# The second MLP matrix of a Fourier-mixer block by seven block products, with the sums in DRAM

## Chip, cores and metric

One core of a Trainium2 chip. The metric is device time of one execution in microseconds (us). The kernel before takes 1678.18 us, the median of three runs (1675.69 to 1680.62).

## The reference, cut to what matters

One layer over 512 tokens of width 2048, batch 1, float32. The change touches the last line but one alone: the product with `w_mlp_out`.

```python
def sqrelu_mlp(h, w1, w2):
    return jnp.square(jax.nn.relu(h @ w1)) @ w2          # 2048 -> 8192 -> 2048
...
y_lat = fourier_mix(h_lat) @ fnet_w_out[slot]            # FFT over tokens and groups of 256
x = x + g1 * rms_norm(y_lat, norm_g[i, 1])
x = x + g2 * rms_norm(sqrelu_mlp(modulate(rms_norm(x, norm_g[i, 2]), sh2, sc2), w_mlp_in[i], w_mlp_out[i]), norm_g[i, 3])
return x
```

## The kernel before

**Three products for one.** Every float32 operand of TensorE is split in two: ScalarE writes a rounded copy `hi` (L115) and VectorE the rest `lo` = source - `hi` (L116). `mm3` (L118 to L121) multiplies hi x lo, lo x hi and hi x hi into one PSUM bank. Weights come by `stream` (L632): a 512 KB load on SP's queue into one of eight buffers `raw`. A weight tile of 128 x 1024 thus costs one load, one CAST on ScalarE and one TENSOR_TENSOR on VectorE.

**First MLP matrix.** The 8192 hidden features are 64 blocks of 128, taken in 32 pairs (units). Pairs 0 to 3 are made together, 4 and 5 by `unit_plain` (L823: 96 matmuls with 512 columns), 6 to 31 by `unit` (L775): token halves, halves of the width and the two blocks of the pair make a 2 x 2 by 2 x 2 block product, which needs seven products (A11, S1, S3, S2, A12, A22, S4) in place of eight, so 168 matmuls with 256 columns, and sums of weights on VectorE (L795, L800, L803, L806). `square_out` (L641) squares on ScalarE and writes the pair's 512 KB from GpSimd's queue to a DRAM tile `gd` (L643).

**Second MLP matrix.** `CHUNKS` cuts the 64 blocks into seven chunks of 8 and two of 4. At a chunk's start `g_in` (L855) loads its pairs back and splits them. For each of the four column groups of 512, 8 blocks x 4 token tiles x 3 = 384 matmuls of 512 columns run per chunk with four PSUM banks; ScalarE copies the banks of chunk 0 into `oacc` (L882), VectorE adds those of the other chunks to it (L884). The last chunk (60, 64) is made token tile by token tile, with the norm and the output behind each (L906 to L928).

**What sets the order.** Each engine runs its instructions in the order in which the program's scheduler put them; an instruction waits for semaphores of other engines and of DMAs. The tile pools have fixed numbers of buffers (8 `raw`, 3 `hi`, 3 `lo`, 6 PSUM banks for products); a buffer that is taken again makes its next writer wait for its last reader. `owed` and `settle` put an eviction off until the next product has been issued.

Of the kernel before, what the change touches and what calls it, by code (L numbers as in the profile page):

```python
# [12 lines left out]
ALU = mybir.AluOpType  # L13
# [42 lines left out]
def block_kernel(ctx: ExitStack, tc, xs, c_l, w_mod, b_col, g_col,  # L56
                 w_in_a, w_in_b, w_in_s, w_out, wf, wf_nyq, fmat_a, fmat_b, csmat, altmat, identm, out):
    nc = tc.nc
# [585 lines left out]

# [178 lines left out]
    def unit_plain(u):  # L823
        pss = []
        for j in range(2):
            ps = bank()
            for half in range(2):
                wr = stream(w_in_b[2 * (u - WAVE // 2) + j, half].rearrange("p k f -> p (k f)"))
                wh, wl = hi4([P, 8, P]), lo4([P, 8, P])
                split(wh, wl, wr.rearrange("p (k f) -> p k f", f=P))  # L830
                for i in range(8):
                    dt = half * 8 + i
                    mm3(ps, wh[:, i, :], wl[:, i, :], hh[dt // 4][:, dt % 4, :], hl[dt // 4][:, dt % 4, :], dt == 0, dt == KT - 1)
            pss.append(ps)
        act_relu2(u, pss)

    for u in range(WAVE // 2, UNIT0):
# [5 lines left out]
        unit_plain(u)  # L843
    for u in range(UNIT0, UNITS):
# [7 lines left out]
    oacc = [x8([P, D]) for _ in range(4)]  # L852
    gts = {}

    def g_in(u):  # L855
        gr = stream(gd[u].rearrange("p f t -> p (f t)"))
        for j in range(2):
            gh, gl = g2k([P, 512], F32R), g2k([P, 512], F32R)
            split(gh, gl, gr[:, j * 512:(j + 1) * 512])
            gts[2 * u + j] = (gh, gl)  # L860

    for c, (f0, f1) in enumerate(CHUNKS):
        for u in range(f0 // 2, f1 // 2):
            g_in(u)
        if c == len(CHUNKS) - 1:
            break
        for n in range(4):
            ns = slice(n * 512, (n + 1) * 512)
            ps = [bank() for _ in range(4)]
            for fb in range(f0, f1, 2):  # L870
                wr = stream(w_out[fb // 2, n].rearrange("p f j -> p (f j)"))
                wh, wl = hi4([P, 2, 512]), lo4([P, 2, 512])
                split(wh, wl, wr.rearrange("p (f j) -> p f j", j=512))
                for i in range(2):
                    fi = fb + i
# [131 lines left out]
```

## Time and profile before

| what | value |
|---|---|
| median of three runs | 1678.18 us (1675.69 to 1680.62) |
| profiled execution, its own time | 1679.38 us |
| span of the profiled execution | 1677.6 us |
| mean granted TensorE clock | 0.992 of full speed |
| matmuls | 10161 |
| HBM read, written | 279.58 MB, 25.17 MB |

The span is what lies between the first and the last instruction of the trace; the execution's own time is 1.8 us longer. Of the views, the shares of busy time tell which engine is full, the chain of waits tells which engine's work the end is made of, the lines tell how long one instruction of a kind takes, the windows tell the same by stage, and the timeline gives start times, from which the spacing of matmuls is read (they are pipelined, so a matmul's own length is more than it costs).

### The profile page before, as it was taken

How to read it: one execution, taken by the hardware profiler on the slowest of the kernel's cores; microseconds unless marked ns; L12 is line 12 of the kernel's file. 1: busy time of each engine (PE TensorE's matmuls, PEld its weight loads, DVE VectorE, ACT ScalarE, POOL GpSimd, SP SyncE). 2: the span in 40 equal slices, each digit the busy share in tenths (PEclk: the TensorE clock that was granted, in tenths of full speed). 3: DMA queues.
4: the chain of work that ended last, by engine and by line, in shares of the span. 5: the costliest groups of instructions: out<-in, count | busy, mean ns of one | idle time of the engine just before them, and what ended most of it. 6: DMA issues, size and time to landing. Idle time of an engine off the chain costs nothing.

```text
span 1677.6 us, 24773 instructions
## 1 busy us (share of the span) xinstructions
PE 1637.5 (98%) x10161; PEld 1392.7 (83%) x10161; DVE 1046.3 (62%) x1417; ACT 658.3 (39%) x989; POOL 22.8 (1%) x46
## 2 busy tenths in 40 slices
PE   6999998999999999999999999999999999999997
PEld 4766654678999999999999988888888888888886
DVE  6777866675988888888777732344343434343557
ACT  6443334335555555454555533222122313221322
POOL 0000000000000000000000000000000000000000
PEclk9999998999999999999999999999999999999999
DMA  9888888886355555554433453424242424342542
GB/s 365 328 299 320 296 306 300 298 312 227 114 177 190 183 179 181 185 177 169 133 126 126 163 164 113 134 98 146 100 143 96 151 99 141 100 150 89 176 149 101
DMA packets 83698, 306.37 MB, mean 183 GB/s; under 512 B 9540, under 2 KB 9556, under 8 KB 82560
## 3 DMA queue, kind: packets, MB, share of 16 engines
q1 hardware_dynamic: 78480, 286.96, 49.7%
q0 software_dynamic: 5104, 17.83, 2.8%
q8 instruction: 79, 1.29, 0.3%
q14 instruction: 35, 0.29, 0.1%
HBM read 279.58 MB, written 25.17 MB: 182 GB/s over the span
## 4 chain that ended last, share of the span: by engine, by line
PE 94%; DMA 3%; DVE 2%; ACT 0%; issue 0%; SPq 0%; DVEq 0%; ACTq 0%
PE ps L119 19%; PE ps L121 18%; PE ps L120 18%; PE ps L789 10%; PE ps L788 10%; PE ps L790 10%; PE mv L202 4%; DMA raw<-in_w_mod 2%; PE mv L168 1%; DMA x<-in_xs 1%; DVE row L217 1%; PE mv L398 0%; PE ps L274 0%; DVE big L485 0%; DVE lo L116 0%
## 5 line engine op out<-in xcount | busy, mean ns | idle before, releaser
L116 DVE TENSOR_TENSOR lo<-raw,hi 128x1024 fp32r<-128x1024 f32 x326 | 398.4, 1223 | 380.4 <-ACT hi L115 370.0
L115 ACT CAST hi<-raw 128x1024 fp32r<-128x1024 f32 x326 | 342.4, 1051 | 593.1 <-PE ps L121 348.5
L119 PE MATMUL ps<-lo,g 128*128 128x512 f32 x1088 | 425.4, 392 | 0.3 <-DVE lo L116 0.3
L120 PE MATMUL ps<-hi,g 128*128 128x512 f32 x1088 | 425.0, 391 | 0.0
L121 PE MATMUL ps<-hi,g 128*128 128x512 f32 x1088 | 421.5, 391 | 0.0
L119 PEld LDWEIGHTS ps<-lo,g 128*128 128x128 f32 x1088 | 204.7, 188 | 49.1 <-issue 3.9
L121 PEld LDWEIGHTS ps<-hi,g 128*128 128x128 f32 x1088 | 204.5, 188 | 46.4 <-issue 4.1
L120 PEld LDWEIGHTS ps<-hi,g 128*128 128x128 f32 x1088 | 204.6, 188 | 43.9 <-issue 1.9
L789 PE MATMUL ps<-big,lo 128*128 128x256 f32 x624 | 177.1, 284 | 0.0
L788 PE MATMUL ps<-big,hi 128*128 128x256 f32 x624 | 176.9, 283 | 0.0
L790 PE MATMUL ps<-big,hi 128*128 128x256 f32 x624 | 176.6, 283 | 0.0
L789 PEld LDWEIGHTS ps<-big,lo 128*128 128x128 f32 x624 | 119.7, 192 | 0.5 <-DVE lo L116 0.2
L788 PEld LDWEIGHTS ps<-big,hi 128*128 128x128 f32 x624 | 119.7, 192 | 0.0
L790 PEld LDWEIGHTS ps<-big,hi 128*128 128x128 f32 x624 | 119.8, 192 | 0.0
L789 PE MATMUL ps<-g,lo 128*128 128x256 f32 x416 | 118.0, 284 | 0.0
L789 PE MATMUL ps<-s,lo 128*128 128x256 f32 x416 | 117.7, 283 | 0.0
L790 PE MATMUL ps<-s,hi 128*128 128x256 f32 x416 | 117.7, 283 | 0.0
L788 PE MATMUL ps<-g,hi 128*128 128x256 f32 x416 | 117.7, 283 | 0.0
L788 PE MATMUL ps<-s,hi 128*128 128x256 f32 x416 | 117.7, 283 | 0.0
L790 PE MATMUL ps<-g,hi 128*128 128x256 f32 x416 | 117.7, 283 | 0.0
L202 PE MATMUL mv<-raw,cst 128*32 128x256 f32 x1088 | 88.9, 406 | 11.1 <-DMA raw<-in_w_mod 7.2
L884 DVE TENSOR_TENSOR x<-x,ps 128x512 f32<-128x512 f32 x112 | 74.6, 685 | 27.7 <-PE ps L121 27.7
(225 smaller groups left out, 2223.7 us busy)
## 6 DMA issues: line engine op xcount, KB each, us to landing
raw<-in_w_mod SPq DMA_DIRECT2D x192, 512.0 KB, 5.2
raw<-in_w_out SPq DMA_DIRECT2D x128, 512.0 KB, 3.5
raw<-in_w_in_s SPq DMA_DIRECT2D x104, 512.0 KB, 3.7
raw<-in_wf SPq DMA_DIRECT2D x32, 512.0 KB, 6.2
gd<-tmp POOLq DMA_DIRECT2D x32, 512.0 KB, 3.1
raw<-gd SPq DMA_DIRECT2D x32, 512.0 KB, 3.2
raw<-in_w_in_a SPq DMA_DIRECT2D x16, 512.0 KB, 4.7
x<-in_xs SPq DMA_DIRECT2D x4, 1024.0 KB, 9.4
```

The source lines that it names most:

```text
L115: nc.scalar.copy(out=hi, in_=src)
L116: nc.vector.tensor_tensor(out=lo, in0=src, in1=as32(hi), op=ALU.subtract)
L119: nc.tensor.matmul(ps, lhsT=ah, rhs=bl, start=start, stop=False)
L120: nc.tensor.matmul(ps, lhsT=al, rhs=bh, start=False, stop=False)
L121: nc.tensor.matmul(ps, lhsT=ah, rhs=bh, start=False, stop=stop)
L168: nc.tensor.matmul(mv[:, 256 + cb:257 + cb], lhsT=rows[:, cb * P:(cb + 1) * P], rhs=ones[:, 0:1], start=True, stop=True)
L202: nc.tensor.matmul(st["ps"][32 * j:32 * j + 32, 0:256], lhsT=cst[:, kq * 4 + j, :], rhs=t[:, j * 256:(j + 1) * 256], start=(kq == 0), stop ...
L217: nc.vector.scalar_tensor_tensor(out=rows, in0=t[:, j * 512:(j + 1) * 512], scalar=sil[:, kt:kt + 1], in1=rows, op0=ALU.mult, op1=ALU.add)
L788: nc.tensor.matmul(ps, lhsT=wh[:, ks], rhs=ll, start=start and k == 0, stop=False, skip_group_check=True)
L789: nc.tensor.matmul(ps, lhsT=wl[:, ks], rhs=lh, start=False, stop=False, skip_group_check=True)
L790: nc.tensor.matmul(ps, lhsT=wh[:, ks], rhs=lh, start=False, stop=k == 7, skip_group_check=True)
L884: nc.vector.tensor_add(out=oacc[t][:, ns], in0=oacc[t][:, ns], in1=ps[t])
```

## The change

Chunks 0 to 6 (pairs 0 to 27) of the second matrix are now made by the same seven block products. The left matrix's 2 x 2 blocks are token halves (`T0`, `T1`) by two halves of the chunk's features; the right one's are feature halves by column halves of 512. For each chunk and each of two column groups `j`, `second(c, j)` makes seven products of 24 matmuls with 512 columns (4 feature blocks x 2 token tiles x 3), so 336 per chunk. Per chunk there are

- 16 weight loads as before (28 splits of weights, since sums of weights are split too), 16 weight sums on VectorE of 128 x 1024;
- 2 loads of 1 MB of activations (`g_chunk`), 4 sums on VectorE for S1, S3, S2, S4 and 7 splits (`left_in`), which serve both `j`; those of the next chunk are issued behind the products that `NEXT` names;
- 28 evictions by ScalarE of 128 x 512 into a ring of six buffers `ev`, and 14 DMAs of 512 KB from GpSimd's queue to 14 DRAM tiles `pacc` (one for each product and `j`). For chunk 0 they are plain, for the six others they add to what is there (`accum_op`): 84 accumulating DMAs.

After the last chunk `gather(j)` loads seven sums of 512 KB and VectorE combines them into `oacc`. Then LAST[0] = (56, 60) runs as a chunk did before, with column groups in the order 0, 2, 1, 3 and `gather(1)` ahead of group 1, and LAST[1] = (60, 64) with the output as before. The pool `bp` of the front is closed before the second matrix and its space goes to three new pools. Pair 31 is made by `unit_plain`, not by `unit`; `gd` now holds four pairs to a tile (the rows that `square_out` writes are 2 KB instead of 4 KB). The host only lays out the weights in another order.

```diff
+PLAIN = tuple(range(WAVE // 2, UNIT0)) + (UNITS - 1,)
+CHUNKS = 7
+LAST = ((56, 60), (60, 64))
...
-    gd = [dp.tile([P, 2, 512], F32, name=f"gd{u}") for u in range(UNITS)]
+    gd = [dp.tile([P, 2, 4, 512], F32, name=f"gd{c}") for c in range(UNITS // 4)]
...
-        nc.gpsimd.dma_start(out=gd[u], in_=r)
+        nc.gpsimd.dma_start(out=gd[u // 4][:, :, u % 4, :], in_=r)
...
+    unit_plain(UNITS - 1)
+    front.close()
+    g4p = ctx.enter_context(tc.tile_pool(name="g4p", bufs=6, reuse_waits="tile"))
+    sbp = ctx.enter_context(tc.tile_pool(name="sbp", bufs=5, reuse_waits="tile"))
+    sap = ctx.enter_context(tc.tile_pool(name="sap", bufs=8, reuse_waits="tile"))
...
+    def g_chunk(c):
+        gf = [s8(True, [P, 4, 512], F32) for _ in range(2)]
+        for j in range(2):
+            nc.sync.dma_start(out=gf[j].rearrange("p u t -> p (u t)"), in_=gd[c][:, j].rearrange("p u t -> p (u t)"))
+        raws[c]["g"] = gf
+    def left_in(c, s):
...
+        a11, a21, a12, a22 = gf[0][:, :, T0], gf[0][:, :, T1], gf[1][:, :, T0], gf[1][:, :, T1]
...
+        elif s == "S1":
+            src = st["v"] = tmp4([P, 4, 256])
+            nc.vector.tensor_sub(out=src, in0=a22, in1=a21)
...
+        t = s8(s in ("A11", "S1", "S3"), [P, 2, 4, 256], F32R)
+        split(t[:, 0], t[:, 1], src)
+        left[c][s] = t
+    def second(c, j):
...
+        def product(s, src):
+            ps = [bank(), bank()]
+            for h in range(2):
+                wh, wl = hi4([P, 1024]), lo4([P, 1024])
+                split(wh, wl, src[h])
+                for k in range(2):
+                    ks = slice(k * 512, (k + 1) * 512)
+                    for i in range(2):
+                        ts = slice(i * P, (i + 1) * P)
+                        t = left[c][s]
+                        mm3(ps[i], t[:, 0, 2 * h + k, ts], t[:, 1, 2 * h + k, ts], wh[:, ks], wl[:, ks], h + k == 0, h + k == 2)
+            settle()
+            def out():
+                ev = g4([P, 2, 512])
+                for i in range(2):
+                    nc.scalar.copy(out=ev[:, i, :], in_=ps[i])
+                if c:
+                    nc.gpsimd.dma_start(out=pacc[s, j], in_=ev, accum_op=ALU.add)
+                else:
+                    nc.gpsimd.dma_start(out=pacc[s, j], in_=ev)
+            owed.append(out)
+            if c + 1 < CHUNKS:
+                for n in NEXT.get((j, s), ()):
+                    left_in(c + 1, n)
+        b11, b12 = load(0), load(1)
+        product("A11", b11)
+        both = [g4([P, 1024]) for _ in range(2)]
+        for h in range(2):
+            nc.vector.tensor_add(out=both[h], in0=b11[h], in1=b12[h])
...
+    NEXT = {(0, "S3"): ("A11",), (0, "A12"): ("S1",), (0, "S4"): ("S3",), (1, "S1"): ("S2",), (1, "S2"): ("A12",),
+            (1, "A12"): ("A22",), (1, "A22"): ("S4",)}
+    for s in PRODUCTS:
+        left_in(0, s)
+    for c in range(CHUNKS):
+        for j in range(2):
+            second(c, j)
+    settle()
...
-    for c, (f0, f1) in enumerate(CHUNKS):
-        for u in range(f0 // 2, f1 // 2):
-            g_in(u)
...
+    gather(0)
+    f0, f1 = LAST[0]
+    for u in range(f0 // 2, f1 // 2):
+        g_in(u)
+    for n in (0, 2, 1, 3):
+        if n == 1:
+            gather(1)
...
+        for t in range(4):
+            nc.vector.tensor_add(out=oacc[t][:, ns], in0=oacc[t][:, ns], in1=ps[t])
```

Up to pair 30 every engine's order is the same as before. Three places differ in a way that the prediction speaks of. In the rows below a name is a tile with its number, `in_...` an input, `sa` and `sb` buffers of the two pools for activations, `e` a buffer of the ring `ev`; DMAHW and DMASW are semaphores of SP's and of GpSimd's transfers. Lines of the changed program are some lines further down (L115 is L118, L116 is L119, L635 is L638).

SP's queue where the second matrix begins, before: the activations of pairs 0 to 3 by four loads, then weights.

```order
L635 DMA raw_9878<-in_w_in_s 128x1024 [waits DMAHW3_49,DVE_49]
L635 DMA raw_10106<-gd_3079 128x1024 [waits DMAHW3_49,DMASW1_49,DVE_49]
L635 DMA raw_10116<-gd_3080 128x1024 [waits DMAHW4_49,DMASW3_49,DVE_49]
L635 DMA raw_10126<-gd_3081 128x1024 [waits DMAHW5_49,DMASW2_49,DVE_49]
L635 DMA raw_10136<-gd_3082 128x1024 [waits DMAHW6_49,DMASW4_49,DVE_49]
L635 DMA raw_10180<-in_w_out 128x1024 [waits DMAHW7_49,DVE_49]
```

And with the change: eight weight loads first, then the activations of chunk 0 (`gd_3079`) and of chunk 1 (`gd_3080`).

```order
L638 DMA raw_9945<-in_w_in_b 128x1024 [waits DMAHW2_49,DVE_49]
L638 DMA raw_10037<-in_w_out_s 128x1024 [waits DMAHW3_49,DVE_49]
...
L638 DMA raw_10172<-in_w_out_s 128x1024 [waits DMAHW2_49,DVE_49]
L878 DMA sa_10004<-gd_3079 128x2048 [waits DMASW3_49,DMASW4_49,DMASW2_49,DMAHW3_49,DMASW1_49,PE_49]
L878 DMA sa_10005<-gd_3079 128x2048 [waits DMAHW4_49]
L878 DMA sa_10163<-gd_3080 128x2048 [waits DMASW7_49,DMASW6_49,DMAHW5_49,DMASW5_49,DMASW0_49]
```

What moved: the first load of activations now also waits for TensorE, since its buffer lies where the first matrix's left operand was, which pair 31's last matmuls read.

VectorE at the same place, with the change: from `lo` of A11's activations (`sa_10008`) to `lo` of the weights of S3's first half (`lo_10128`).

```order
L119 TENSOR_TENSOR sa_10008<-sa_10004,sa_10008 128x1024 [waits DMAHW3_49,Activation_49]
L892 TENSOR_TENSOR tmp_10011<-sa_10005,sa_10004 128x1024 [waits DMAHW4_49,DMASW0_49]
L895 TENSOR_TENSOR tmp_10016<-sa_10004 128x1024 [waits DMASW1_49]
L119 TENSOR_TENSOR sa_10013<-tmp_10011,sa_10013 128x1024 [waits Activation_49]
L119 TENSOR_TENSOR sa_10018<-tmp_10016,sa_10018 128x1024 [waits Activation_49]
L898 TENSOR_TENSOR tmp_10011<-tmp_10011,sa_10004 128x1024 [waits DVE_49]
L119 TENSOR_TENSOR lo_10104<-e_10078,hi_10103 128x1024 [waits Activation_49]
L119 TENSOR_TENSOR sb_10022<-tmp_10011,sb_10022 128x1024 [waits Activation_49]
L119 TENSOR_TENSOR sb_10025<-sa_10005,sb_10025 128x1024 [waits Activation_49]
L901 TENSOR_TENSOR tmp_10011<-tmp_10011,sa_10005 128x1024 [waits DVE_49]
L119 TENSOR_TENSOR sb_10028<-sa_10005,sb_10028 128x1024 [waits Activation_49]
...
L119 TENSOR_TENSOR lo_10128<-raw_10039,hi_10127 128x1024 [waits PE_49,Activation_49]
```

Two rows are left out, both on chunk 1's activations; before the change two TENSOR_TENSOR of 128 x 512 for each of chunk 0's four pairs stood there. What moved: thirteen operations of the new left operands stand between A11's activations and S3's weights.

VectorE where `gather(1)` ends, with the change: its last operations ahead of the evictions (L1020) of LAST[0]'s first column group.

```order
L980 SCALAR_TENSOR_TENSOR sb_14326<-raw_14488,raw_14492 128x512
L978 SCALAR_TENSOR_TENSOR sa_14323<-raw_14490,raw_14494 128x512 [waits DMAHW3_49]
L119 TENSOR_TENSOR lo_14455<-raw_14452,hi_14454 128x1024 [waits Activation_49]
L978 SCALAR_TENSOR_TENSOR sa_14324<-raw_14490,raw_14494 128x512
L979 TENSOR_TENSOR sb_14325<-raw_14488,raw_14498 128x512 [waits DMAHW4_49]
L979 TENSOR_TENSOR sb_14326<-raw_14488,raw_14498 128x512
L1020 TENSOR_TENSOR sa_14323<-sa_14323,ps_14350 128x512 [waits PE_49]
```

What moved: the combination of the second seven sums, which did not exist before, stands ahead of a weight's `lo` and of the first evictions.

## Rows read from the trace of the kernel before

**Rows 1.** The page: busy time by engine, and the chain that ended last.

```profile
PE 1637.5 (98%) x10161; PEld 1392.7 (83%) x10161; DVE 1046.3 (62%) x1417; ACT 658.3 (39%) x989; POOL 22.8 (1%) x46
...
PE 94%; DMA 3%; DVE 2%; ACT 0%; issue 0%; SPq 0%; DVEq 0%; ACTq 0%
```

**Rows 2.** Windows inside the second matrix: span, then each engine's busy time, clock, DMA.

```profile
core 0: us, PE busy (x) PEld busy (x) DVE busy (x) ACT busy (x) POOL busy (x), PEclk, DMA share, GB/s
1076.00:1152.00 76.00, 76.00 (x337) 62.94 (x336) 32.62 (x38) 18.84 (x22) 0.00 (x0) 1.00 0.38 125
```

**Rows 3.** Timeline of PE where the second matrix begins: start, length, instruction.

```profile
970.55 0.28 PE L789 MATMUL ps<-g,lo 128*128 128x256 f32 x1
970.67 0.28 PE L790 MATMUL ps<-g,hi 128*128 128x256 f32 x1
970.79 0.40 PE L119 MATMUL ps<-lo,g 128*128 128x512 f32 x1
```

**Rows 4.** Timeline of PE where the last chunk begins, after 2880 matmuls.

```profile
1623.62 0.39 PE L119 MATMUL ps<-big,g 128*128 128x512 f32 x1
```

**Rows 5.** Lines of the window 971 to 1624: count, busy, mean ns, idle before.

```profile
L116 DVE TENSOR_TENSOR lo<-raw,hi 128x1024 fp32r<-128x1024 f32 x118 | 144.6, 1225 | 295.6 <-ACT hi L115 285.6 <-DMA raw<-in_w_out 9.9
L115 ACT CAST hi<-raw 128x1024 fp32r<-128x1024 f32 x118 | 124.2, 1053 | 357.8 <-PE ps L121 305.6 <-DVE x L884 48.2 <-DMA raw<-in_w_out 3.9
L884 DVE TENSOR_TENSOR x<-x,ps 128x512 f32<-128x512 f32 x112 | 74.6, 685 | 27.7 <-PE ps L121 27.7
L882 ACT COPY x<-ps 128x512 f32<-128x512 f32 x16 | 9.4, 589 | 8.3 <-PE ps L121 7.3
```

**Rows 6.** Loads of 1 MB: issue on SP, landing times of `x`, and medians by group.

```profile
L142 SPq DMA_DIRECT2D x<-in_xs x4: 421/473/1011, 1.2 to 3.6; - x4
...
DMA to landing us min/median/max: 5.0/11.9/16.2
...
x<-in_xs SPq DMA_DIRECT2D x4, 1024.0 KB, 9.4
```

**Rows 7.** Timeline of VectorE inside the first matrix.

```profile
561.17 1.22 DVE L803 TENSOR_TENSOR raw<-raw,raw 128x1024 f32<-128x1024 f32 x1
562.31 0.74 DVE L217 SCALAR_TENSOR_TENSOR row<-raw,sil,row 128x512 f32<-128x512 f32 x1
...
565.50 1.23 DVE L116 TENSOR_TENSOR lo<-raw,hi 128x1024 fp32r<-128x1024 f32 x1
566.76 1.22 DVE L806 TENSOR_TENSOR raw<-raw,raw 128x1024 f32<-128x1024 f32 x1
```

**Rows 8.** Windows in the first matrix, and waits there: total, times, longest.

```profile
500.00:576.00 76.00, 76.00 (x636) 76.00 (x636) 66.17 (x74) 38.98 (x53) 2.13 (x4) 1.00 0.53 182
...
DVE lo L116 <- ACT hi L115: 25.0, 33, 1.4
```

**Rows 9.** Windows around a stretch in which TensorE had idled.

```profile
120.00:123.00 3.00, 0.98 (x24) 0.39 (x16) 3.00 (x6) 2.97 (x7) 0.00 (x0) 1.00 0.95 351
123.00:126.00 3.00, 3.00 (x17) 2.33 (x10) 3.00 (x8) 0.00 (x0) 0.00 (x0) 0.61 1.03 415
126.00:129.00 3.00, 3.00 (x12) 2.36 (x12) 1.53 (x3) 0.62 (x2) 0.00 (x0) 0.83 1.03 412
```

**Rows 10.** The page: GpSimd's DMA queue, and landings of 512 KB in three stages.

```profile
q0 software_dynamic: 5104, 17.83, 2.8%
...
raw<-in_w_mod SPq DMA_DIRECT2D x192, 512.0 KB, 5.2
...
gd<-tmp POOLq DMA_DIRECT2D x32, 512.0 KB, 3.1
raw<-gd SPq DMA_DIRECT2D x32, 512.0 KB, 3.2
```

**Rows 11.** GpSimd's lines: issue of the 512 KB write, mean ns.

```profile
L643 POOL DMA_DIRECT2D gd<-tmp x32 | 17.1, 534 | 772.0 <-ACT tmp L642 768.3 <-DVE lo L116 3.7
```

More of the change, by code (lines that the diff above doesn't have):

```diff
@@ L827, in unit_plain @@
             for half in range(2):
[L828 removed]
+                wr = stream(w_in_b[2 * PLAIN.index(u) + j, half].rearrange("p k f -> p (k f)"))
                 wh, wl = hi4([P, 8, P]), lo4([P, 8, P])
@@ L843, in block_kernel @@
         unit_plain(u)
-    for u in range(UNIT0, UNITS):
+    for u in range(UNIT0, UNITS - 1):
         if u >= 8:
@@ L850, in block_kernel, with g4, s8 @@
     settle()
-    oacc = [x8([P, D]) for _ in range(4)]
+    unit_plain(UNITS - 1)
[3 more added lines that the diff above has]
+    sap = ctx.enter_context(tc.tile_pool(name="sap", bufs=8, reuse_waits="tile"))
+    def g4(shape, dt=F32):
+        return g4p.tile(shape, dt, tag="g4", bufs=6, name=nm("e"))
+    def s8(first, shape, dt):
+        if first:
+            return sap.tile(shape, dt, tag="sa", bufs=8, name=nm("sa"))
+        return sbp.tile(shape, dt, tag="sb", bufs=5, name=nm("sb"))
@@ new lines, in block_kernel @@
+    PRODUCTS = ("A11", "S1", "S3", "S2", "A12", "A22", "S4")
+    pacc = {(s, j): dp.tile([P, 2, 512], F32, name=f"p{s}{j}") for s in PRODUCTS for j in range(2)}
+    left = [{} for _ in range(CHUNKS)]
+    raws = [{} for _ in range(CHUNKS + 1)]
+    def g_chunk(c):
[3 more added lines that the diff above has]
+        raws[c]["g"] = gf
@@ new lines, in second, with load @@
+    def second(c, j):
+        def load(b):
+            return [stream(w_out_s[c, j, b, h].rearrange("p k n -> p (k n)")) for h in range(2)]
+        def product(s, src):
[16 more added lines that the diff above has]
+                    nc.gpsimd.dma_start(out=pacc[s, j], in_=ev, accum_op=ALU.add)
+                else:
+                    nc.gpsimd.dma_start(out=pacc[s, j], in_=ev)
[8 more added lines that the diff above has]
+            nc.vector.tensor_add(out=both[h], in0=b11[h], in1=b12[h])
+        b22 = load(2)
+        product("S1", both)
+        for h in range(2):
+            nc.vector.tensor_add(out=b12[h], in0=b12[h], in1=b22[h])
+        product("S3", b12)
+        b21 = load(3)
+        for h in range(2):
+            nc.vector.tensor_add(out=b11[h], in0=b12[h], in1=b11[h])
+        product("S2", b11)
+        product("A12", b21)
+        for h in range(2):
+            nc.vector.tensor_add(out=b12[h], in0=b11[h], in1=b21[h])
+        product("A22", b12)
+        product("S4", b22)
@@ new lines, in block_kernel, with gather @@
+    oacc = []
+    def gather(j):
+        p = {}
+        for s in ("A11", "S2", "A12", "S1", "S4", "S3", "A22"):
+            p[s] = stream(pacc[s, j].rearrange("p i n -> p (i n)"))
+        if not oacc:
+            oacc.extend(s8(i < 2, [P, D], F32) for i in range(4))
+        left_c, right_c = slice(j * 512, (j + 1) * 512), slice(1024 + j * 512, 1536 + j * 512)
+        add = nc.vector.tensor_add
+        u2, v = p["S2"], p["A11"]
+        nc.vector.tensor_sub(out=u2, in0=p["A11"], in1=p["S2"])
+        for i in range(2):
+            h = slice(i * 512, (i + 1) * 512)
+            add(out=oacc[i][:, left_c], in0=p["A11"][:, h], in1=p["A12"][:, h])
+        w = p["A12"]
+        add(out=w, in0=u2, in1=p["S1"])
+        add(out=u2, in0=u2, in1=p["S3"])
+        for i in range(2):
+            h = slice(i * 512, (i + 1) * 512)
+            nc.vector.scalar_tensor_tensor(out=oacc[i][:, right_c], in0=w[:, h], scalar=-1.0, in1=p["S4"][:, h], op0=ALU.mult, op1=ALU.subtract)
+            add(out=oacc[2 + i][:, left_c], in0=u2[:, h], in1=p["A22"][:, h])
+            nc.vector.scalar_tensor_tensor(out=oacc[2 + i][:, right_c], in0=u2[:, h], scalar=-1.0, in1=p["S1"][:, h], op0=ALU.mult, op1=ALU.subtract)
@@ L887, in block_kernel @@
-    f0, f1 = CHUNKS[-1]
+            gts[2 * u + j] = (gh[:, j, :], gl[:, j, :])
+    gather(0)
[5 more added lines that the diff above has]
+            gather(1)
+        ns = slice(n * 512, (n + 1) * 512)
+        ps = [bank() for _ in range(4)]
+        for fb in range(f0, f1, 2):
+            wr = stream(w_out[fb // 2 - CHUNKS * 4, n].rearrange("p f j -> p (f j)"))
+            wh, wl = hi4([P, 2, 512]), lo4([P, 2, 512])
+            split(wh, wl, wr.rearrange("p (f j) -> p f j", j=512))
+            for i in range(2):
+                fi = fb + i
+                gh, gl = gts[fi]
+                for t in range(4):
+                    ts = slice(t * P, (t + 1) * P)
+                    mm3(ps[t], gh[:, ts], gl[:, ts], wh[:, i, :], wl[:, i, :], fi == f0, fi == f1 - 1)
+        for t in range(4):
+            nc.vector.tensor_add(out=oacc[t][:, ns], in0=oacc[t][:, ns], in1=ps[t])
@@ L888, in block_kernel @@
+    f0, f1 = LAST[1]
+    for u in range(f0 // 2, f1 // 2):
+        g_in(u)
     wos = {}
@@ L890, in block_kernel @@
         for n2 in range(2):
-            wh, wl = big([P, 2, 2, 512], F32R), big([P, 2, 2, 512], F32R)
+            wh, wl = (s8(fb == f0 or n2 == 0, [P, 2, 2, 512], F32R) for _ in range(2))
             for i in range(2):
-                wr = stream(w_out[fb // 2, 2 * n2 + i].rearrange("p f j -> p (f j)"))
+                wr = stream(w_out[fb // 2 - CHUNKS * 4, 2 * n2 + i].rearrange("p f j -> p (f j)"))
                 split(wh[:, i], wl[:, i], wr.rearrange("p (f j) -> p f j", j=512))
```

69 lines of the change are left out of this document (35 added, 34 removed).

## The prediction

> **What bounds the kernel now.** Read the busy shares and the chain of waits first: TensorE is busy 98% of the span and holds 94% of the chain [rows 1]. Nothing but fewer matmuls, or cheaper ones, can make this kernel much faster; anything that makes TensorE wait costs in full. Then read a window in the stage that is changed: TensorE is full, at clock 1.00, the higher of its two levels (2.4 GHz), while VectorE works 32.62 us of 76, ScalarE 18.84, and the DMA engines 38% of the time [rows 2]. That idle time is what the change spends. Last, the price of a matmul comes from start times, not from lengths. The second matrix starts at 970.79 [rows 3] and its last chunk at 1623.62 [rows 4]; 2880 matmuls lie between, so (1623.62 - 970.79) / 2880 = 0.2267 us for one with 512 columns, with no stall in it. One with 256 columns costs 0.12 us (970.55, 970.67, 970.79) [rows 3].
>
> The sum below stands against the profiled execution, 1679.4 us; it is 1.2 us above the median of 1678.2, well inside the spread of the runs. A difference under 0.3% (5 us) can't be told from no change.
>
> **What goes.** Seven chunks lose 48 matmuls each (384 to 336): 336 x 0.2267 = **-76.2 us**, all on TensorE's path.
>
> **Pair 31.** 168 x 0.12 = 20.2 us become 96 x 0.2267 = 21.8: **+1.6**. The 2 KB rows that GpSimd writes change nothing that TensorE waits for: the pairs of a chunk are written long before it is read, save pair 31, which is read last.
>
> **The start of the second matrix.** Before, it begins one matmul step behind the first matrix [rows 3], since the activations were loaded early. Now the first load of activations waits for pair 31's last matmuls (the excerpt of SP's queue), and TensorE has nothing else to do. The path is: issue 0.47, landing of 1 MB 5.0 at the fastest, both of `x` [rows 6], CAST 1.05 and subtraction 1.22 [rows 5], together 7.7 us. I take the fastest landing because the queues are nearly empty there; the 9.4 median belongs to the start of the program, where everything loads at once, and is the upper bound. Then VectorE is late: thirteen operations of 128 x 1024 stand between A11's activations and S3's first weights (the excerpt of VectorE). One costs between 1.14 us (561.17 to 562.31) and 1.26 (565.50 to 566.76) from start to start [rows 7]; I take 1.17, so 15.2 and some 0.3 for waits. TensorE has A11 and S1 to do meanwhile, 48 x 0.2267 = 10.9, and waits 4.6. Eight more operations (9.4) stand ahead of the second half of S2, against 36 matmuls (8.2): 1.2 more. Together **+13.5**; 8 if the load's path were all (VectorE on time), 22 with the slow landing and all of ScalarE's casts in line. After idling, TensorE ran three us at 0.61 and three at 0.83 of its clock [rows 9]; here that falls into time in which it waits for VectorE anyway, so it is put at nothing, and would be 1.7 us if VectorE were on time.
>
> **Inside the chunks.** VectorE gets, per chunk, 28 weight subtractions, 16 weight sums, 7 subtractions and 4 sums for the left operands: 55 x 1.17 = 64.4 us of 336 x 0.2267 = 76.2, or 84%. In the first matrix it worked 66.17 us of 76 (87%) and TensorE still did 76.00 of 76.00; it waited for ScalarE at most 1.4 us [rows 8]. ScalarE gets 35 casts and 28 copies, 35 x 1.053 + 28 x 0.589 = 53.4 us [rows 5]. So neither is full, and only the order can hurt. Behind the first product of a chunk's second column group the next activations may be loaded only once A11's reader is done, and seven left-hand operations stand ahead of S1's weights: 8.2 against 24 to 36 matmuls (5.4 to 8.2). I put each of the six boundaries at 1.5 us, half of what is between nothing and the worst case's 3 or so: **+9**, with 0 and 30 as ends (30 is a 1 MB landing of 9.4 instead of 5.0 at each boundary, 4.4, and some more).
>
> **The accumulating DMAs.** The trace of before holds none. The plain write of 512 KB from GpSimd is the nearest row: 17.83 MB took 2.8% of the DMA engines' span, 47 us [rows 10], so 1.38 us of all sixteen for 0.524 MB. Per chunk 10.5 MB are loaded (8.4 of weights, 2.1 of activations), at the 412 GB/s of the dense stretch [rows 9] 25.5 us; with 14 x 1.38 = 19.3 that is 45 of 76 us. That is the lower end, and below it no gain is possible, since nothing was there before. For the upper end take the slowest 512 KB row of a busy stage, 5.2 us to land [rows 10], as if each accumulation kept all sixteen engines for so long: it decides a rival below. I take something near the lower end, up to two or three plain writes, because the sums are wanted only a chunk later and six buffers with nine uses per 38 us give each a landing of some 20 us before ScalarE waits: 0 in the sum. GpSimd issues 14 per chunk at 0.534 [rows 11], 7.5 us of 76.
>
> The Trainium skill ("Collectives: The Full Stack", section "The bandwidth ceiling: the fold count and why AG ≠ RS ≠ AR") says that an addition in the DMA path runs at about half of a copy's rate since it needs two source reads. No row here can show it; by it an accumulation would be an estimated 2.8 us of all engines, and the sum would stay as it is, at a smaller chance for the rival below.
>
> **The end.** After the last S4, TensorE waits for two copies (2 x 0.59), three casts of activations and weights (3 x 1.05) and one subtraction (1.22) [rows 5], **+5.6**, since the evictions stand ahead of the casts on ScalarE. The clock falls once behind this, **+1.7** [rows 9]. `gather(1)` stands ahead of the first evictions (third excerpt), some 14 operations, 10 us; LAST[0]'s matmuls (192 x 0.2267 = 43.5) cover it, as six banks are there. One cast ahead of the last chunk: **+1.1**. The tail is as it was.
>
> **The sum.** -76.2 + 1.6 + 13.5 + 9 + 5.6 + 1.7 + 1.1 = -43.7, so 1679.4 - 43.7 = **1636 us**.
>
> **Rivals.**
> *The DMA engines become the bound (slower).* Place: the ring `ev` of six buffers. If accumulations take long, ScalarE's copies wait for a free buffer, the PSUM banks stay full and TensorE stops, in chunks 1 to 6. The chunk may last 76.2 + 43.7 / 6 = 83.5 before the gain is gone; less 25.5 for the loads that leaves 58 / 14 = 4.1 us for each, three plain writes. At 5.2 it is 14 x 5.2 + 25.5 = 98.3, so 22 x 6 = 133 us more: about 1768. For it: nothing measured prices an addition with its read of DRAM. Against it: a plain write needs 1.38, the landing of 3.1 to 3.2 in this stage [rows 10] is mostly latency, and even twice or three times the work fits. 13 in 100.
> *The order on VectorE hurts more.* At 84% with in-order queues, each weight sum that waits for a late load holds the subtractions behind it. With 4 us more at each of six boundaries, about 1660. For it: in the first matrix left operands were ready beforehand; here they mix in. Against it: 87% without a stall [rows 8]. 18 in 100.
> *The gain is eaten almost whole,* by both together in a milder form: within 5 us of now, 3 in 100. That the change does not do what it says can't be: the order lists 408 matmuls fewer, 336 + 72 for pair 31.
>
> **How the numbers follow.** The forecast has 66 in 100: faster. With the second rival it makes 84 for faster, 3 for the same, 13 for slower. The range: all low ends together, start 8, boundaries 0, end 2.6 instead of 8.4, give 1636 - 5.5 - 9 - 5.8 = 1616; the high ends, start 22, boundaries 30 and some 4 more at the end, 1636 + 8.5 + 21 + 4 = 1670. It holds the forecast and the second rival; the other cases, 16 in 100, lie outside.
>
> **What would show it.** Matmul starts 0.2267 apart inside the chunks and 76 us from one chunk's A11 to the next, up to 78; TensorE idle some 8 us behind pair 31, released by the subtraction behind a load of `gd`, then some 5 us at S3, released by VectorE; idle some 6 us behind the last S4; VectorE busy about 64 us per chunk; accumulations landing within 20 us and no ScalarE copy waiting for a DMA. Wrong if chunk 0, whose writes are plain, lasts 76 us and chunks 1 to 6 much longer with copies released by GpSimd's DMAs (the first rival), or if TensorE's waits inside the chunks end with VectorE and sum to over 30 us (the second).

## The result, and the profile after

| | before | after |
|---|---|---|
| median | 1679.31 us (4 runs) | 1656.16 us (4 runs, 1652.97 to 1658.15) |
| ratio after / before | | 0.9864, 95% interval 0.9841 to 0.9887 |
| profiled execution, its own time | 1679.38 us | 1652.97 us, span 1651.2 |
| mean granted clock | 0.992 | 0.984 |

The change gains 23.2 us by the medians and 26.4 by the profiled executions, not the 43.7 forecast; 1656 lies inside the range, 20 us above the predicted 1636. The page of after, against [rows 1, 10]: busy times, GpSimd's DMA queue, the chain, and landings of the accumulations and of the loads of activations.

```profile
PE 1578.7 (96%) x9753; PEld 1333.5 (81%) x9753; DVE 1261.3 (76%) x1545; ACT 855.6 (52%) x1235; POOL 106.1 (6%) x144
...
q0 software_dynamic: 19216, 69.22, 19.3%
...
PE 77%; issue 9%; DMA 6%; DVE 6%; ACT 1%; POOL 0%; DVEq 0%; SPq 0%; POOLq 0%; ACTq 0%
...
pS<-e POOLq DMA_DIRECT2D x56, 512.0 KB, 6.0
pA<-e POOLq DMA_DIRECT2D x42, 512.0 KB, 6.3
...
sa<-gd SPq DMA_DIRECT2D x14, 1024.0 KB, 6.8
```

TensorE issues the 408 matmuls fewer that the order promised, but its part of the chain falls from 94% to 77%: the path now runs through other engines at places. To find them, set the stage against its matmuls. From pair 31's last matmul to the last of the program there are 7 x 336 + 2 x 192 = 2736 matmuls, 2736 x 0.2267 = 620.2 us if nothing stalled. The two ends, in the timeline of PE (start, length, instruction, and in brackets the idle time before it with its releaser):

```profile
971.27 0.39 PE L124 MATMUL ps<-big,hi 128*128 128x512 f32 x1
...
1640.55 0.39 PE L124 MATMUL ps<-sb,e 128*128 128x512 f32 x1
```

1640.55 - 971.27 - 620.2 is **49 us lost**, where the forecast had 13.5 + 9 + 8.4 = 30.9. That is the whole difference: pair 31 ended 1.1 us earlier than the forecast's 970.8 + 1.6, and 1636 + (49.0 - 30.9) - 1.1 is 1653, the profiled time. The tail is as it was. By the gaps between matmul starts over 0.2267, the 49 are: start 16.2, boundaries 13.9, end 16.6, and 2.3 in gaps of 0.3 us and less, spread over the chunks.

**The start.** PE, then SP's queue and VectorE, from pair 31's last matmul on, and windows of the same stretch (columns as in [rows 2]):

```profile
977.30 1.22 PE L122 MATMUL ps<-lo,sa 128*128 128x512 f32 x2 [5.64 <-ACT sa L118]
...
991.80 0.39 PE L124 MATMUL ps<-hi,sa 128*128 128x512 f32 x1
997.20 0.80 PE L122 MATMUL ps<-lo,sa 128*128 128x512 f32 x1 [5.01 <-DVE lo L119]
```

```profile
971.23 2.03 SPq L878 DMA_DIRECT2D sa<-gd  x4
```

```profile
979.41 1.22 DVE L892 TENSOR_TENSOR tmp<-sa,sa 128x1024 f32<-128x1024 f32 x1 [0.44 <-DMA sa<-gd]
983.28 1.22 DVE L895 TENSOR_TENSOR tmp<-sa 128x1024 f32<-128x1024 f32 x1 [2.64 <-DMA gd<-tmp]
...
995.92 2.35 DVE L119 TENSOR_TENSOR lo<-raw,hi 128x1024 fp32r<-128x1024 f32 x2
```

```profile
977.00:983.00 6.00, 5.19 (x11) 3.65 (x12) 3.20 (x3) 1.30 (x2) 0.00 (x0) 0.50 1.01 401
983.00:989.00 6.00, 5.89 (x26) 4.51 (x24) 5.72 (x5) 2.98 (x4) 0.00 (x0) 1.00 0.25 104
```

The load of activations is issued when pair 31's matmuls end, 971.23, as the order said; the first matmul starts 6.0 us after pair 31's last one, S3's first at 997.20. VectorE works through the thirteen operations with one large gap: L895, the difference for S3, waits 2.64 us for pair 31's own write to DRAM, because the buffer `tmp` that it fills is still being read by that write. A11 ran at clock 0.50, the lower level (1.2 GHz), after TensorE's 5.64 us idle; VectorE set S3's start all the same.

The write itself was slow: GpSimd issued it at 973.67, just behind the four loads of 1 MB (the activations of chunks 0 and 1), while the DMA engines were full (1.01 in the window from 977). Landings of the 32 writes of the first matrix, then of pair 31's alone:

```profile
DMA to landing us min/median/max: 3.1/3.7/9.6
...
DMA to landing us min/median/max: 9.6/9.6/9.6
```

Landing in the median 3.7, it would have been done at an estimated 977.4, before VectorE came to L895. In e2 below, with two of the four loads, it landed in 7.2 us, and in e4, where the loads were issued some 10 us ahead of it, in 4.4 at most; in neither did L895 wait for it.

**The boundaries.** PE and VectorE where chunk 2 follows chunk 1, and the window behind it beside that of the boundary before:

```profile
1149.57 0.39 PE L124 MATMUL ps<-hi,sa 128*128 128x512 f32 x1
1151.83 0.50 PE L122 MATMUL ps<-lo,sa 128*128 128x512 f32 x1 [1.87 <-DVE lo L119]
```

```profile
1147.15 1.22 DVE L119 TENSOR_TENSOR sa<-tmp,sa 128x1024 fp32r<-128x1024 f32 x1
1148.29 1.22 DVE L119 TENSOR_TENSOR sb<-tmp,sb 128x1024 fp32r<-128x1024 f32 x1
1149.42 1.22 DVE L945 TENSOR_TENSOR raw<-raw,raw 128x1024 f32<-128x1024 f32 x1
1150.56 1.22 DVE L119 TENSOR_TENSOR lo<-e,hi 128x1024 fp32r<-128x1024 f32 x1
```

```profile
1071.00:1075.00 4.00, 3.33 (x8) 2.67 (x9) 4.00 (x5) 0.61 (x1) 0.61 (x1) 0.60 0.74 130
1151.00:1155.00 4.00, 3.17 (x14) 2.63 (x15) 4.00 (x4) 1.12 (x2) 0.73 (x1) 1.00 0.95 157
```

VectorE has no idle time here; it does splits of left operands (`sa`, `sb`) and a sum for S3's weights (L945), and S1's weight, L119 into `lo`, comes behind them. The same 1.87 us stands behind the first product, A11, of chunks 1 to 5 (and not of 6, where no more left operands are made). Behind two of the five, at chunks 1 and 3, the clock fell (the windows: 0.60 at chunk 1, 1.00 at chunk 2), so the five cost 3 x 2.14 + 2 x 3.74 = 13.9 us, from matmul start to matmul start.

**The end.** SP's queue, ScalarE, VectorE and PE where `gather(0)` and LAST[0] follow the last chunk of seven products, and windows of the same stretch:

```profile
1532.40 0.61 SPq L638 DMA_DIRECT2D raw<-gd  x1
...
1537.67 0.53 SPq L638 DMA_DIRECT2D raw<-gd  x1
```

```profile
1546.44 1.99 ACT L118 CAST e<-raw 128x1024 fp32r<-128x1024 f32 x2 [2.38 <-DMA raw<-gd]
```

```profile
1524.90 1.29 DVE L972 TENSOR_TENSOR sa<-raw,raw 128x512 f32<-128x512 f32 x2 [2.65 <-DMA raw<-pA]
...
1536.42 1.23 DVE L975 TENSOR_TENSOR raw<-raw,raw 128x1024 f32<-128x1024 f32 x1 [2.91 <-DMA raw<-pS]
...
1547.51 2.36 DVE L119 TENSOR_TENSOR e<-raw,e 128x1024 fp32r<-128x1024 f32 x2 [6.33 <-ACT e L118]
```

```profile
1538.83 0.50 PE L122 MATMUL ps<-lo,sb 128*128 128x512 f32 x1 [2.25 <-DVE lo L119]
...
1551.06 0.79 PE L122 MATMUL ps<-lo,e 128*128 128x512 f32 x1 [7.62 <-DVE lo L119]
```

```profile
1530.00:1540.00 10.00, 7.52 (x30) 5.33 (x29) 6.24 (x9) 2.22 (x3) 0.85 (x1) 0.97 1.01 290
1540.00:1550.00 10.00, 3.44 (x10) 2.32 (x8) 3.67 (x5) 4.74 (x6) 0.84 (x1) 0.67 1.04 347
```

The seven sums of `gather(0)` take load buffers `raw` while chunk 6 still runs. VectorE stands in line for sums (2.65, 2.91 us), so chunk 6's last weights are late (1.09, 0.23 and 2.25 us of idle PE), and LAST[0]'s activations, `raw<-gd`, are issued only at 1532.40 and 1537.67. They land 7.6 and 8.7 us later, where the median of this load before was 3.2 [rows 10], while the DMA engines are full (1.01 and 1.04 in the windows). Their casts begin at 1546.44, and TensorE idles 7.62 us. Of the 16.6 us of the end 11.2 are idle time; nearly all of the rest is matmuls at the lower clock, behind the waits of 2.25 and 7.62.

**The accumulations** keep nobody waiting inside the chunks: ScalarE's copies into the ring wait for TensorE alone (waits of ScalarE, 1076 to 1535: total, times, longest), though the DMA engines are nearly full (windows of two chunks):

```profile
ACT e L927 <- PE ps L124: 76.0, 78, 1.2
```

```profile
1063.00:1143.00 80.00, 78.13 (x337) 63.94 (x336) 63.82 (x56) 51.28 (x64) 11.55 (x14) 0.98 0.85 219
1143.00:1222.00 79.00, 77.13 (x338) 62.77 (x337) 63.97 (x56) 51.44 (x64) 11.91 (x14) 1.00 0.90 226
```

### The profile page after: what moved, and what is told of

Same layout as the page of the kernel before. It is cut to its first block, busy times and chain, and to the rows that moved or that the text cites. A ratio compares the mean times of both kernels' runs of the same rounds, so it can differ in the third digit from the quotient of the medians.

```text
span 1651.2 us, 24701 instructions
## 1 busy us (share of the span) xinstructions
PE 1578.7 (96%) x9753; PEld 1333.5 (81%) x9753; DVE 1261.3 (76%) x1545; ACT 855.6 (52%) x1235; POOL 106.1 (6%) x144
## 3 DMA queue, kind: packets, MB, share of 16 engines
q0 software_dynamic: 19216, 69.22, 19.3%
## 4 chain that ended last, share of the span: by engine, by line
PE 77%; issue 9%; DMA 6%; DVE 6%; ACT 1%; POOL 0%; DVEq 0%; SPq 0%; POOLq 0%; ACTq 0%
PE ps L122 15%; PE ps L124 14%; PE ps L123 14%; PE ps L792 9%; PE ps L791 9%; PE ps L793 9%; DMA raw<-in_w_mod 4%; PE mv L205 4%; DVE lo L119 1%; DMA raw<-pS 1%; PE mv L171 1%; DVE row L220 1%; DVE sb L119 1%; DMA raw<-gd 1%; DMA x<-in_xs 1%
## 5 line engine op out<-in xcount | busy, mean ns | idle before, releaser
L119 DVE TENSOR_TENSOR lo<-raw,hi 128x1024 fp32r<-128x1024 f32 x379 | 461.0, 1222 | 180.4 <-ACT hi L118 179.2
L118 ACT CAST hi<-raw 128x1024 fp32r<-128x1024 f32 x379 | 398.1, 1051 | 342.0 <-PE ps L793 190.0
L122 PE MATMUL ps<-lo,sb 128*128 128x512 f32 x448 | 176.3, 394 | 3.6 <-DVE lo L119 3.6
L124 PE MATMUL ps<-hi,sb 128*128 128x512 f32 x448 | 175.2, 391 | 0.0
L123 PE MATMUL ps<-hi,sb 128*128 128x512 f32 x448 | 175.1, 391 | 0.0
L791 PE MATMUL ps<-big,hi 128*128 128x256 f32 x600 | 170.3, 284 | 0.0
L793 PE MATMUL ps<-big,hi 128*128 128x256 f32 x600 | 170.0, 283 | 0.0
L927 ACT COPY e<-ps 128x512 f32<-128x512 f32 x196 | 114.9, 587 | 102.9 <-PE ps L124 95.6
L122 PE MATMUL ps<-lo,sa 128*128 128x512 f32 x336 | 134.8, 402 | 20.3 <-DVE lo L119 14.6
L123 PE MATMUL ps<-hi,sa 128*128 128x512 f32 x336 | 133.7, 398 | 0.5 <-DVE sa L119 0.5
L124 PE MATMUL ps<-hi,sa 128*128 128x512 f32 x336 | 133.2, 396 | 0.0
L791 PEld LDWEIGHTS ps<-big,hi 128*128 128x128 f32 x600 | 115.2, 192 | 0.0
L793 PEld LDWEIGHTS ps<-big,hi 128*128 128x128 f32 x600 | 115.2, 192 | 0.0
L122 PEld LDWEIGHTS ps<-lo,sb 128*128 128x128 f32 x448 | 84.5, 189 | 24.6 <-DVE lo L119 7.1
```

Of the source, the lines that this page charges most:

```text
L118: nc.scalar.copy(out=hi, in_=src)
L119: nc.vector.tensor_tensor(out=lo, in0=src, in1=as32(hi), op=ALU.subtract)
L122: nc.tensor.matmul(ps, lhsT=ah, rhs=bl, start=start, stop=False)
L123: nc.tensor.matmul(ps, lhsT=al, rhs=bh, start=False, stop=False)
L124: nc.tensor.matmul(ps, lhsT=ah, rhs=bh, start=False, stop=stop)
L791: nc.tensor.matmul(ps, lhsT=wh[:, ks], rhs=ll, start=start and k == 0, stop=False, skip_group_check=True)
```

## Experiments

The order up to pair 30 is the same in all of these, yet pair 31 ends anywhere from 969.5 to 979.9 us in their profiled executions; why the part before it varies was not studied. So each kernel is judged by its ratio and by the loss of its stage: its last matmul, less pair 31's last, less 620.2, split as above.

| run | ratio (95%) | median us | lost us | start | boundaries | end |
|---|---|---|---|---|---|---|
| after | 0.9864 (0.9841 to 0.9887) | 1656.16 | 49.0 | 16.2 | 13.9 | 16.6 |
| e11_change_again | 0.9872 (0.9852 to 0.9891) | 1656.88 | 50.8 | 16.8 | 13.9 | 17.5 |
| e1_plain | 0.9838 (0.9819 to 0.9858) | 1648.39 | 44.0 | 16.5 | 13.9 | 11.1 |
| e2_left_once | 0.9717 (0.9694 to 0.9740) | 1627.41 | 26.2 | 10.3 | 0 | 15.6 |
| e3_gather_late | 0.9820 (0.9792 to 0.9847) | 1646.26 | 43.0 | 16.4 | 13.9 | 10.2 |
| e4_slot | 0.9867 (0.9836 to 0.9897) | 1652.93 | 46.7 | 12.5 | 13.9 | 18.2 |
| e5_in_turn | 0.9785 (0.9764 to 0.9805) | 1641.94 | 32.2 | 14.2 | 2.9 | 14.8 |
| e6_gather_behind | 0.9787 (0.9759 to 0.9815) | 1640.78 | 35.2 | 16.6 | 13.9 | 2.6 |
| e7_all | 0.9682 (0.9660 to 0.9704) | 1624.95 | 16.8 | 9.4 | 2.9 | 4.1 |
| e9_all_a11 | 0.9670 (0.9654 to 0.9686) | 1623.70 | 16.8 | 9.4 | 2.8 | 4.4 |
| e10_all_plain | 0.9647 (0.9632 to 0.9662) | 1619.41 | 15.1 | 9.3 | 2.8 | 2.6 |
| e8_two_sums | 1.0470 (1.0444 to 1.0495) | 1755.70 | 148.8 | | | |

The theory: what the forecast missed is order. Work that is wanted later stands on in-order engines, and in load buffers, ahead of what TensorE wants next. The rival: the accumulating DMAs, which fill the DMA engines to 85 to 90%, make everything late. e11 is the change once more, and shows how far the stage varies by itself: 1.8 us between these two executions.

> The changed kernel itself, on the same chip and beside the same runs of the kernel before, for the difference to the two others: ratio 0.984 to 0.989.

**e1_plain: every DMA to the sums plain.**

```diff
-                    nc.gpsimd.dma_start(out=pacc[s, j], in_=ev, accum_op=ALU.add)
+                    nc.gpsimd.dma_start(out=pacc[s, j], in_=ev)
```

> All 98 sums are written by plain DMAs instead of 84 accumulating ones; the output then holds only the last chunk's products, nothing else is left out. In the changed kernel GpSimd's queue took 19.3% of the span, which makes about 3.0 us of all sixteen DMA engines for one accumulation against 1.38 for a plain write. Theory A (waits on VectorE's order and on buffers): the DMA engines are full but not on the path; the time falls by 0 to 4 us from 1656, the waits at the chunk boundaries (13.9 us) and at the end (16.6) stay. Rival B (the accumulations delay the loads behind those waits): both waits shrink by half or more, 15 to 25 us faster, 1631 to 1641.

Measured 44.0 lost, 5 to 7 less than the change's two executions (the median is 7.8 lower): more than the theory's 0 to 4, far less than the rival's 15 to 25. Start and boundaries did not move. GpSimd's queue on the page of e1, and the landings of L929's DMAs, of e1 first and then of after:

```profile
q0 software_dynamic: 19216, 69.22, 10.9%
```

```profile
DMA to landing us min/median/max: 2.9/4.2/8.1
```

```profile
DMA to landing us min/median/max: 4.9/6.3/10.9
```

In e1, 0.109 x 1646.4 us over 69.22 / 0.524 = 132 DMAs is 1.36 us of all sixteen engines for a plain one. In after, 0.193 x 1651.2 = 318.7, less the 132 - 84 = 48 plain ones, leaves (318.7 - 48 x 1.36) / 84 = 3.0 for an accumulation. The rival holds at one place: with plain writes the sums of `gather(0)` arrive sooner, and the small waits ahead of LAST[0] (1.09, 0.23, 2.25) shrink to one of 0.94; the large one stays (7.86). Of the 5.5 us that the end gains on after, 2.4 are waiting; the rest is matmuls that no longer run at the lower clock.

**e2_left_once: the left operands of chunk 0 used for all chunks.**

```diff
+                left[c + 1] = left[0]
+            if False:
                 for n in NEXT.get((j, s), ()):
                     left_in(c + 1, n)
```

> The left operands are made for chunk 0 only and used for all seven chunks; left out are the loads of activations, 11 VectorE operations and 7 casts per chunk for chunks 1 to 6, so the product is not the reference's. Theory A: VectorE's backlog of left-hand operations sets the 1.9 us wait at each boundary; the boundaries lose nothing (less than 2 us in all against 13.9), 12 to 15 us faster, 1641 to 1644; the start (16 us) and the end (16.6) stay. Rival B (DMA engines): only 2 of 10.5 MB of loads per chunk go; boundaries shrink by a third, 3 to 6 us faster.

The boundaries vanish here with the accumulations in place, and in e1 they stayed without them, so it was not the accumulations that made them. The start, expected to stay, gains 5.9, as chunk 1's operations and loads are no longer mixed into it; the end keeps its loss. What is left of TensorE's waits in the stage of e2:

```profile
PE ps L122 <- DVE lo L119: 12.2, 5, 6.0
PE ps L122 <- ACT sa L118: 5.6, 1, 5.6
```

This run also takes eleven operations, some 13 us, off VectorE in each chunk, and the loads of activations, so it cannot tell order from load; e5 does.

**e5_in_turn: the next chunk's left operands held behind the split of the product that `NEXT` names.** `issue_after` is an edge for the scheduler: here ScalarE's and VectorE's work on the left operands may not be put ahead of that split.

```diff
-                for n in NEXT.get((j, s), ()):
-                    left_in(c + 1, n)
+                with tc.issue_after(a), tc.issue_after(v):
+                    for n in NEXT.get((j, s), ()):
+                        left_in(c + 1, n)
```

> Each left operand's operations are tied behind the weights of the product that names it, by an order edge on ScalarE and on VectorE; the work is the same. In the changed kernel they ran about a chunk ahead of their need and in a heap: 4 of them stand ahead of S1's weights at each chunk's start. Theory A: this order makes the 1.9 us wait and the clock's fall behind it; the five boundaries lose under 2 us in all (13.9 before), and S3's wait at the start of the second matrix shrinks by 2 to 3 us since two operations of chunk 1 go behind it: 14 to 17 us faster, ratio to the kernel before 0.976 to 0.978. Rival B (late loads): no change.

The boundaries fall from 13.9 to 2.9, six of 0.48. VectorE does the same operations as in after (1545), and the loads and accumulations are the same; only the turn differs. That shows the cause of the boundaries.

**e3_gather_late: `gather(0)` behind LAST[0]'s first column group, ahead of its additions.**

```diff
-    gather(0)
...
+        if n == 0:
+            gather(0)
```

> The combination of the first seven sums is written behind the first matmuls of the chunk (56, 60), after its own activation and weight loads. Theory A: the loads of seven sums take seven of eight load buffers and VectorE waits in line for them, which makes TensorE 16.6 us late around the last products; with the loads of activations and weights ahead, 6 to 12 us of it go, 1644 to 1650. Rival B (the DMA engines are full there by accumulations and sums): the same bytes move, 0 to 3 us.

The end falls from 16.6 to 10.2, not to nothing: the place in the text alone does not decide. VectorE of e3 still meets a sum ahead of the subtraction for the activations, and TensorE waits 5.2 us for that:

```profile
1541.18 1.23 DVE L974 TENSOR_TENSOR raw<-raw,raw 128x1024 f32<-128x1024 f32 x1 [1.98 <-DMA raw<-pS]
...
1544.66 2.35 DVE L119 TENSOR_TENSOR e<-raw,e 128x1024 fp32r<-128x1024 f32 x2
```

**e6_gather_behind: both gathers behind a column group's matmuls, and held behind the subtractions of LAST[0]'s activations and weights.**

```diff
+        if n < 2:
+            with tc.issue_after(v), tc.issue_after(gv[0]):
+                gather(n)
```

> As in the run with the late combination, and VectorE's operations of the combination are tied behind the activations and weights of the group they follow. Theory A: in the run before, the remaining wait at the end (9.8 us) came from two activation subtractions queued behind a combination that waited for its sums; with the order forced TensorE loses 4 to 7 us at the end, ratio 0.977 to 0.982. Rival B (DMA engines full at the end): the loss stays near 10, ratio 0.982.

The end falls to 2.6 us, 14.0 less, and nothing else moves. With the accumulations still there, what the gathers put ahead of LAST[0] was most of the end's loss. The edit moves the sums' loads, their buffers and VectorE's additions together, so it does not tell apart which of the three cost how much.

**e4_slot: a one-column memset takes one buffer of 1 MB at the second matrix's start,** so that the first load of activations gets a buffer that pair 31's matmuls don't read.

```diff
+    nc.gpsimd.memset(s8(True, [P, D], F32)[:, 0:1], 0.0)
     for s in PRODUCTS:
         left_in(0, s)
```

> A buffer is burnt ahead of chunk 0 (one small memset by GpSimd), so that the first activations load into space that pair 31 does not read, and can be loaded 20 us earlier. Theory A: TensorE's wait at the start of the second matrix falls from 5.6 us to about 2 (A11's own buffer still waits for pair 31, then cast and subtraction), but S3 still waits, since VectorE's operation on S3's left operand waits for pair 31's write to DRAM: 2 to 4 us faster in all. Rival C (the load is the whole cost of the start): 8 to 14 us faster.

The start falls by 3.7. The ratio, 0.9867, shows none of it: the end takes 0.7 to 1.6 us back (18.2 against 17.5 and 16.6), and the interval is wider than what is left, 2.3 us in the stage. L895 no longer waits for pair 31's write, against the expectation; VectorE of e4:

```profile
987.48 1.22 DVE L892 TENSOR_TENSOR tmp<-sa,sa 128x1024 f32<-128x1024 f32 x1
988.61 1.22 DVE L895 TENSOR_TENSOR tmp<-sa 128x1024 f32<-128x1024 f32 x1
```

**e7_all: e4, e5 and e6 together,** and L895's difference in a buffer that pair 31's write does not read.

```diff
+            src = st["v"] = (tmp4 if c else g4)([P, 4, 256])
```

> The burnt buffer, another buffer for S3's difference of chunk 0 (so that it no longer waits for pair 31's write), the left operands in turn and the combination tied behind: the work is the same. Theory A: start 16 to about 8 us, boundaries 14 to 2, end 17 to 6; together 30 us faster than the change, ratio 0.966 to 0.972. Rival B: DMA engines set the pace and only a part comes, ratio 0.976 or more.

Lost 16.8, 32.2 less than the change; e4, e5 and e6 alone had 2.3, 16.8 and 13.8 less, together 32.9, so the parts add up nearly. At 1624.95 us it beats both kernels.

**e9_all_a11: e7 with A11's copies of chunk 0 in the other pool's buffers.**

```diff
-        t = s8(s in ("A11", "S1", "S3"), [P, 2, 4, 256], F32R)
+        t = s8(s in ("S1", "S3") or (s == "A11" and c > 0), [P, 2, 4, 256], F32R)
```

> As the run with all four edits, and A11's left operand of chunk 0 goes to the pool of which the first buffer was not read by pair 31, so its cast and subtraction need not wait for TensorE. Theory A: the first wait of 2.7 us and the fall of the clock behind it go; the start loses 3 to 5 us in place of 9.4, ratio to the kernel before 0.963 to 0.967. Rival (VectorE is late for S3 anyway, so the wait only moves there): the start loses 7 to 9 us, ratio 0.967 to 0.969.

The stage is as in e7, 16.8, the start still 9.4, so neither the theory's 3 to 5 nor the rival's 7 to 9 came, and the first wait stays 2.71 us. ScalarE of e9 tells why:

```profile
974.36 0.60 ACT L653 ACTIVATE tmp<-ps 128x512 f32<-128x512 f32 x1 [4.38 <-PE ps L125]
974.99 1.06 ACT L646 ACTIVATE tmp<-tmp 128x1024 f32<-128x1024 f32 x1
975.95 1.03 ACT L118 CAST sb<-sa 128x1024 fp32r<-128x1024 f32 x1
```

The cast is held by its place behind pair 31's evictions, not by its buffer.

**e10_all_plain: e9 with plain DMAs.**

> As the run before, with plain DMAs for the accumulating ones; the output holds only the last chunk's products, nothing else is left out. It prices the accumulations once the order no longer hides them. Theory A (the accumulations stay beside TensorE's work): 0 to 2 us faster than with them. Rival B: over 5 us.

Against e9 the stage gains 1.7 us, at the end (4.4 to 2.6). The medians differ by 4.3 us, between the theory's 0 to 2 and the rival's over 5, and the intervals of the two ratios overlap. With the order mended the rival is worth some 2 us in the stage.

**e8_two_sums: each result accumulated into a second set of DRAM tiles too,** so 28 DMAs per chunk.

```diff
                     nc.gpsimd.dma_start(out=pacc[s, j], in_=ev, accum_op=ALU.add)
+                    nc.gpsimd.dma_start(out=pextra[s, j], in_=ev, accum_op=ALU.add)
```

> Each result is also accumulated into a second set of 14 DRAM tiles that nothing reads: 28 accumulations per chunk in place of 14. If one keeps all sixteen DMA engines for 3.0 us, a chunk needs 28 x 3.0 + 25.5 = 110 us of them against 76 of TensorE: some 30 us more in each of six chunks, about 1830 to 1850. If the cost is mostly latency that overlaps, under 1720.

Measured 1755.7 us: the mechanism came, its size was overrated. A window of e8 over one chunk, and the waits for the ring on ScalarE (1258 to 1450):

```profile
1258.00:1354.00 96.00, 81.81 (x338) 66.03 (x338) 64.46 (x56) 50.39 (x63) 24.01 (x28) 0.93 1.06 263
```

```profile
ACT e L928 <- DMA qS<-e: 25.5, 4, 6.5
```

The DMA engines are full, the copies into the ring wait for them, and a chunk takes 96 us. With the forecast's 25.5 for its loads that is an estimated (96 - 25.5) / 28 = 2.5 us for an accumulation at full load, less than the 3.0 read from the queue's share; that share in e8, 30.2% for 230 DMAs of which 168 add, gives 2.65 in the way of e1. The forecast's slower case, the ring held up by the DMAs, thus exists, but reaches TensorE by another way than described. More waits of the same stretch:

```profile
PE ps L122 <- DVE lo L119: 30.4, 6, 8.2
ACT hi L118 <- DVE e L944: 28.8, 6, 6.6
DVE e L944 <- DMA qS<-e: 14.9, 4, 6.4
```

VectorE's sums of S1's weights (L944) go into buffers of the same ring; they wait for its DMAs, and the casts and subtractions of these weights stand behind them. All of TensorE's waits here end with VectorE's `lo`, none with a bank that ScalarE emptied late. The change stays short of this, at 14 x 3.0 + 25.5 = 67.5 us of a chunk's 79.

## Why the prediction was right in sign and too low

**Right.** The 336 matmuls at 0.2267 and pair 31's 1.6 stand: the loss above is measured against them and accounts for the whole time. VectorE's ledger stands: forecast 64.4 us per chunk, measured 63.8 to 64.0; ScalarE 53.4 against 51.3 to 51.4. The accumulations at 0 inside the chunks stand: no copy waited for a DMA. Their price lay between the two bounds, 1.38 and 5.2, and inside "two or three plain writes"; 2.5 to 3.0 is under the 4.1 from which the first rival decides.

The Trainium skill ("Collectives: The Full Stack", section "The bandwidth ceiling: the fold count and why AG ≠ RS ≠ AR") tells of ring collectives that the step that adds runs at half the rate of the step that copies, because the addition reads two sources. The ratio here is near that: 2.5 to 3.0 is 1.8 to 2.2 times a plain write's 1.36. No run here shows that the second read is the reason.

**"Together +13.5", the start: 16.2.** The mechanism was right, a size off. The forecast has S3's first matmul 7.7 + 4.6 us late; by the trace it is 997.20 - 971.27 - 49 x 0.2267 = 14.8, 2.5 more, and L895's wait of 2.64 for pair 31's write is of that size. The step counted the thirteen operations and "some 0.3 for waits", without asking what their buffers last held, and took the queues for nearly empty, where four loads of 1 MB came together ahead of that write. So pair 31's write did hold TensorE up, through VectorE; the forecast asked only when it is read. The load's path was shorter than 7.7, as TensorE began 6.0 us behind pair 31: its first matmul waited for the cast alone, so the 1.22 of the subtraction did not belong in the path. That bought nothing, since VectorE set S3's start. The 1.2 at S2 did not come; a second fall of the clock, behind the wait of 5.01, took 1.5 in its place.

**"Each of the six boundaries at 1.5, +9": 13.9.** The second rival in a mild form. The forecast's own cause, left operands ahead of S1's weights, was the right one, though it looked for it behind the first product of a chunk's second column group, and the waits came behind the first product of the chunk; its size was half of a guessed worst case. It is 2.14 five times, and the clock behind two of them adds 1.6 each. That a matter of order, and not VectorE's load, made them, e5 shows.

**"The end, +5.6 +1.7 +1.1": 16.6. This step failed.** It counted ScalarE's and VectorE's work between the last S4 and LAST[0], and priced `gather(1)`, which is covered: after the wait that ends at 1551.06 TensorE has none left, so the 1.1 ahead of the last chunk did not come either. `gather(0)`, which stands earlier and takes load buffers, DMA time and VectorE's turn, was not priced at all. e6 took 14.0 us of the end away by moving the gathers alone. The accumulations, put at 0 in the whole sum, cost 5.5 to 6.4 us here, by e1, and 1.7 once the order is mended, by e10.

**The range.** Its upper end, 1670, was made mostly of slow landings at the start and at the boundaries; neither occurred. The result lies inside it by other terms, which is luck in part.

## What to carry to other kernels

When an engine's spare time is spent on work wanted a stage later, its share of busy time (here 64 of 79 us) does not tell whether TensorE will wait: read, at each seam, what stands in the in-order queues and in the shared load buffers ahead of the next operand, and what the buffers that change hands there last held. Of the 49 us that this change lost, 32 came back by order and buffers alone. An accumulating DMA to DRAM can carry block sums off the path if about twice a plain write's engine time fits beside the loads, and if what reads the sums does not stand ahead of what TensorE needs next.

## What the runs showed of the hardware

- An accumulating DMA of 512 KB from SBUF to DRAM takes an estimated 2.5 us (e8, all engines full) to 3.0 us (after) of the sixteen DMA engines, a plain one 1.36 (e1), and lands in 6.3 us (median) where the plain one lands in 4.2. DMA engines 85 to 90% busy still cost TensorE nothing inside the chunks: the boundaries are 13.9 with plain writes too.
- The clock fell to the lower level behind two of five waits of 1.87 us on TensorE that look alike in the trace; what made the difference is open.
- An operation of 1.22 us on VectorE waited 2.64 us for a 512 KB write to DRAM by another engine's queue, through a buffer that it took over. That write landed in 9.6 us behind four loads of 1 MB; the median of its kind was 3.7.
